# Four of down's low weight parts formed on GpSimd, and four reorderings ahead of them, in a decoder layer

## The chip, the cores and the metric

The kernel runs on one core of a Trainium2 chip. The metric is the device time of one execution in microseconds (us); the kernel before took 369.11 us in the median of three runs (368.17 to 369.8). A core has a matrix engine (TensorE, in the rows PE, its weight loads PEld), a vector engine (VectorE, DVE), a scalar engine (ScalarE, ACT), GpSimd (POOL) and a queue engine (SyncE, SP) that issues most DMAs. Each engine executes its own instructions in program order and waits on semaphores for the others.

## The reference

One layer over x (256 tokens x 1024), in float32:

```
z = x @ w_in;  u = z[:, :512];  q, k, v = thirds of z[:, 512:]     # 8 heads of 64
pool = causal window means of u (2, 4, 8, 16) - u, times w_pool, times pool_scale
attn = causal softmax(q k^T / 8) v
h1 = layer_norm(a*x + concat(pool, attn) @ w_out)                  # a = 2^(1/4)
cross = softmax((h1 @ w_xq) (mem @ w_xk)^T / 16) (mem @ w_xv)      # 4 heads of 256, 256 memory tokens
h2 = layer_norm(a*h1 + cross @ w_xo)
out = layer_norm(a*h2 + (silu(h2 @ w_gate) * (h2 @ w_up)) @ w_down)  # inner width 2816
```

## The kernel before

**Three products for one.** TensorE multiplies in a float32 form of fewer bits (F32R). So each operand is kept as two parts: a high part, which ScalarE casts, and a low part, which VectorE forms as the operand minus its high part. A product is three matmuls: high by high, high by low, low by high (`three`, L353 to L358). A matmul of 128x512 or 128x256 outputs adds into one of eight PSUM banks: a ring of four for long accumulations (`accbank`) and a ring of four for the rest (`bank`). A bank comes free when the engine that reads its former content has done so.

**The weight stream.** All weights pass through one `Stream`, as numbered items (w0 to w138) in the order of use. For an item SyncE's queue loads a raw tile (7 buffers), ScalarE casts the high part (L146, L160) and VectorE subtracts the low part (L148, L161); high and low tiles have 9 buffers. The program order on ScalarE, VectorE and SyncE is fixed when the kernel is built: every call of `ws.get` in the generator of a projection first makes sure that its own item is prepared, and, unless `ws.held` is set, prepares one item more, up to 9 ahead of what is used. With `ws.pace` at n only every n-th call does so. A raw buffer is loaded anew only after its low part has been formed, and the load stands in SyncE's order right behind the preparation that frees it.

**The stages, in order.** q and k (w0 to w10), v, u, the keys of the memory (`do_xk`, w19 to w26), the output projection `mix` (w27 to w34) with the first layer norm, the values of the memory (`do_xv`, w35 to w42), the four heads of cross-attention (`do_xq`, `xscores`, `xattend`), their output projection with the second layer norm, eleven chunks of gate and up (`proj_n`, c = 0 to 10), and down. The generators yield after each step of k, and `run(gen, n)` takes n steps, so that the softmax, pooling and splits of other parts are put between them by hand.

**Keys of the memory.** `do_xk` makes four chunks in 64 steps, and after each chunk splits the accumulator into xkT (ScalarE, then VectorE, through `split`, L418 to L420). The bank of its last chunk is the one in which the fourth accumulator of `mix` begins. The last steps stand so:

```
run(xk, 6)        # L688
mix_pool(2)
mix_pool(3)
run(xk, 6)
run(xk)
```

**Scores of a head.** `xscores` (L847) makes for two token halves and two slices of the head the three products each, in the order high by high, high by low, low by high; the low part of the query is written by VectorE (`split_scaled`, L424).

**First gate/up chunk.** Before chunk 0 the tokens of h2 are turned on TensorE and split into h2T; `proj_n` (L380) for the first token half begins as soon as that is there.

**Down.** For the first 9 of 11 chunks (SEVEN = 9) down is done on two-by-two blocks with seven products instead of eight: weight sums (`sums`) and token sums (GpSimd, L968 to L973) are formed, four products are shared over the chunks (`shared_products`) and three are added on (`four`, `fourth`). After the last gate/up chunk `down` runs: the single-row weights w121 to w134 (`c_t4`, `c_low`), then the last two chunks, w135 to w138, for each of the four output pieces in turn (L1154 to L1156). The pieces 1 and 2 get the shared sums added by VectorE before they begin (L1144). In between `events` puts the splits of the last tokens and the merging of the shared sums (L1116 to L1125). The third layer norm and the stores follow.

Of the kernel before, what the change touches and what calls it, by code (L numbers as in the profile page):

```python
# [14 lines left out]
P = 128  # L15
D = 1024
S = 256
T = S // P
KD = D // P
# [16 lines left out]
SEVEN, LAG, LATE = 9, 2, 4  # L36


def r32(t):
    return t.bitcast(F32)  # L40


class Stream:


    def __init__(self, nc, pool):
        self.nc, self.pool = nc, pool
        self.src, self.raws, self.tiles, self.homes = [], [], [], []
        self.loads, self.splits = {}, {}
        self.used, self.held = 0, True  # L50
        self.pace, self.asked = 1, 0
        self.cuts, self.steps = {}, {}
        self.items, self.freed, self.rest = [], 0, {}
        self.kept = set()

    def add(self, src, parts=2):

# [71 lines left out]
    def prepare(self, upto, now=False):  # L129
        nc = self.nc  # L130
        while len(self.tiles) < min(upto, len(self.items)):
            i = len(self.tiles)
            kind, r = self.items[i]
            if kind == "sums" and upto < i + 2 and not now:
                break
            for split in self.splits.pop(i, []):
                split()
            if kind == "whole":
                self.fetch(r + 1, nc.sync)
                raw = self.raws[r]  # L140
                hi = self.pool.tile(list(raw.shape), F32R, tag="hi", name=f"w{i}h")
                lo = self.pool.tile(list(raw.shape), F32R, tag="lo", name=f"w{i}l")
                whole = [slice(0, raw.shape[2])]
                casts, subs = self.steps.get(r, (whole, whole))
                for s in casts:
                    nc.scalar.copy(hi[:, :, s], raw[:, :, s])  # L146
                for s in subs:
                    nc.vector.tensor_sub(lo[:, :, s], raw[:, :, s], r32(hi[:, :, s]))  # L148
                self.tiles.append((hi, lo))
                self.freed = r + 1  # L150
            elif kind == "sums":
                self.fetch(r + 2, nc.sync)
                self.tiles += self.sums(i, r)
                self.freed = r + (1 if r in self.kept else 2)
            else:
                raw, (hi, lo) = r(), self.part(i)
                self.freed += len(self.kept)
                self.kept.clear()
                s = slice(0, raw.shape[2])
                nc.scalar.copy(hi[:, :, s], raw)  # L160
                nc.vector.tensor_sub(lo[:, :, s], raw, r32(hi[:, :, s]))  # L161
                self.tiles.append((hi, lo))
            self.fetch(max(self.freed, len(self.homes)) + RAW_BUFS, nc.sync)

    def next(self):

        i = len(self.tiles)
        return i + (2 if i < len(self.items) and self.items[i][0] == "sums" else 1)
# [28 lines left out]
def decoder_layer(  # L197
# [3 lines left out]
    nc = tc.nc  # L201
# [11 lines left out]
    def a8(name, dt=F32):  # L213
        return ap.tile([P, KD, S], dt, tag="a8", name=name)

    def bank(name):
        return pb.tile([P, 512], F32, tag="b", name=name)

    def accbank(name):
        return pa.tile([P, 512], F32, tag="acc", name=name)  # L220


    ws = Stream(nc, wp)
# [8 lines left out]
    def block(w, at, shape):  # L232

        j, n = shape
        return w[at:at + P * j * n].rearrange("(p j n) -> p j n", p=P, j=j)

    c_qk = []
    for k in range(KD):
        if k < 3:
            first = [ws.add(block(w_qkv, (2 * k + j) * P * 512, (1, 512)), 1)[0] for j in range(2)]  # L240
# [13 lines left out]
    def row(k):  # L254

        return w_down[k * P:(k + 1) * P].rearrange("(k p) n -> p k n", p=P)
# [10 lines left out]
    c_gu, c_sums = [], []  # L267
    for c in range(NFC):
        c_gu.append(ws.add(w_gu[c], 4))
        n = c - LAG  # L270
        if 0 <= n < SEVEN:
            c_sums.append(ws.add_sums([row(2 * n), row(2 * n + 1)], (lambda n=n: t4_home(n)) if n < SEVEN - 1 else None))
    c_t4, c_low = {}, {}
    c_t4[SEVEN - 1] = ws.add_home(lambda: ws.rest[ws.items[c_sums[-1][0][0]][1]]())
    c_low[SEVEN - 1] = ws.add(row(2 * SEVEN - 1), 1)
    for n in range(0, SEVEN - 1, 2):
        home = lambda n=n: t4[n // 2]
        if n < LATE:
            c_t4[n] = ws.add_home(home)
        for c in (n, n + 1):  # L280
            c_low[c] = ws.add(row(2 * c + 1), 1)
        if n >= LATE:
            c_t4[n] = ws.add_home(home)
    c_dn = {c: [ws.add(row(2 * c + f), 1) for f in range(2)] for c in range(SEVEN, NFC)}


# [66 lines left out]
    def three(ps, w, y, start, stop, part=False):  # L353

        (wa, wb), (ya, yb) = w, y
        nc.tensor.matmul(ps, wa, ya, start=start, stop=False, skip_group_check=part)  # L356
        nc.tensor.matmul(ps, wa, yb, start=False, stop=False, skip_group_check=part)  # L357
        nc.tensor.matmul(ps, wb, ya, start=False, stop=stop, skip_group_check=part)  # L358

    def pair(hl, *ix):  # L360
        return hl[0][ix], hl[1][ix]

    ALL = slice(None)
# [13 lines left out]
                    ws.done(numbers, k)  # L377
                yield

    def proj_n(pss, numbers, yT, last=True):  # L380

        for k in range(KD):
            for t, ps in pss.items():
                three(ps, pair(yT, ALL, k, slice(t * P, (t + 1) * P)), ws.get(numbers, k), k == 0, k == KD - 1)
            if last:
                ws.done(numbers, k)
            yield
# [22 lines left out]
    def run(gen, n=None):  # L410

        while n is None or n > 0:
            if next(gen, gen) is gen:
                return False
            n = None if n is None else n - 1
        return True
# [201 lines left out]
    def mix_pool(g):  # L618
        pm = bank("pm")
        nc.tensor.matmul(pm[:, :S], wpl[:, g, :], upad[:, g, PADW:], start=True, stop=True)  # L620
        nc.scalar.activation(cT[0][:, g, :], pm[:, :S], AF.Copy, bias=0.0, scale=psc[:, g:g + 1])
        nc.vector.scalar_tensor_tensor(cT[1][:, g, :], pm[:, :S], psc[:, g:g + 1],
                                       r32(cT[0][:, g, :]), op0=OP.mult, op1=OP.subtract)


    def do_v():
        pieces = [(t, 0, 512) for t in range(T)]
        acc = {piece: accbank("pv") for piece in pieces}
        yield from proj_rows(acc, c_v, lambda k: (xT[0][:, k], xT[1][:, k]), pieces, True, True, True)
        for piece in pieces:  # L630
            nc.scalar.copy(vt[:, piece[0], :], acc[piece])

    def do_u():
        for c in range(2):
            ps = accbank("pu").rearrange("p (f t) -> p f t", f=2)
            yield from proj_t([ps[:, f, :] for f in range(2)], c_u[c], xT)
            nc.scalar.copy(upad[:, 2 * c:2 * c + 2, PADW:], ps)
            for f in range(2):
                windows(2 * c + f)

    xkT = (a8("xkTh", F32R), a8("xkTl", F32R))

    def do_xk():
        for c in range(4):
            ps = accbank("pxk").rearrange("p (f t) -> p f t", f=2)
            yield from proj_t([ps[:, f, :] for f in range(2)], c_xk[c], mT)
            split(xkT[0][:, 2 * c:2 * c + 2, :], xkT[1][:, 2 * c:2 * c + 2, :], ps)

    v, u, xk = do_v(), do_u(), do_xk()
# [38 lines left out]
    run(xk, 6)  # L688
    mix_pool(2)
    mix_pool(3)  # L690
    run(xk, 6)
    run(xk)
    ws.pace = 1


# [56 lines left out]
    PIECES = tuple((t, *half) for t in range(T) for half in HALVES)  # L752
# [62 lines left out]
    xv = [ap.tile([P, T, D], F32R, tag="a8", name=f"xv{i}") for i in range(2)]  # L815

    def do_xv():
        acc = {piece: (bank if piece == PIECES[3] else accbank)("xv") for piece in PIECES}
        yield from proj_rows(acc, c_xv, lambda k: (mT[0][:, k], mT[1][:, k]),
                             PIECES, True, True, True)  # L820
        xvs.update(acc)
# [17 lines left out]
    xqT, xpr, xpt, turnsx = {}, {}, {}, {}  # L839
# [6 lines left out]

    def xscores(h):  # L847
        ps = bank("xs").rearrange("p (t s) -> p t s", t=2)
        for t in range(T):
            for kk in range(2):  # L850
                three(ps[:, t, :], pair(xqT[h], ALL, kk, slice(t * P, (t + 1) * P)), pair(xkT, ALL, 2 * h + kk),
                      kk == 0, kk == 1)
        pr = sp.tile([P, 2, T, P], F32, name="xpr", tag="pr", bufs=PR_BUFS)
        by_t = pr.rearrange("p s t b -> p t s b")
        scaled(by_t, exps(by_t, ps.rearrange("p t (s b) -> p t s b", s=2), negmax(ps)))
        xpr[h] = pr
# [68 lines left out]
    h2T = (a8("h2Th", F32R), a8("h2Tl", F32R))  # L925
# [94 lines left out]
    first = [accbank("pg") for t in range(T)]  # L1020
    second = [accbank("pg") for t in range(T)]
    gu1 = [proj_n({t: second[t]}, c_gu[1], h2T, t == 1) for t in range(T)]
    run(proj_n({0: first[0]}, c_gu[0], h2T, False))
    transpose_tok(h2T, h2[:, 1, :], 1, 0)
    run(gu1[0], 2)
    gated(0, 0, first[0])
# [11 lines left out]
    acc = {}  # L1038
# [8 lines left out]
    for c in range(1, NFC):  # L1047
        sgs.append(sp.tile([P, 2, T, P], F32, name="sg", tag="pr", bufs=PR_BUFS))
        pss = {t: second[t] if c == 1 else accbank("pg") for t in range(T)}
# [236 lines left out]
```

## Time and profile before

| | |
|---|---|
| median of three runs | 369.11 us (368.17 to 369.8) |
| the profiled execution | 369.07 us, span of its instructions 367.1 us |
| TensorE busy | 361.8 us, 99% of the span |
| VectorE busy | 309.8 us, 84% |
| ScalarE busy | 198.4 us, 54% |
| GpSimd busy | 68.1 us, 19% |
| granted TensorE clock | full (1.0, the level of 2.4 GHz) over the span |

The span is the time from the first to the last instruction of the program; the execution's own time has 1.9 us more around it. A timeline row gives start and duration of an instruction in us, the engine, the line of the kernel, the operation, output<-inputs, shapes, and in brackets the idle time of the engine just before it and what ended that. Matmuls are pipelined: durations overlap, and the step from one start to the next is what a matmul costs, 0.23 us for 128x512 and 0.12 us for 128x256. Vector instructions overlap a little too: a low part of 128x1024 lasts 1.22 us, and the next starts 1.13 us after it.

### The profile page before, as it was taken

To read this page: it belongs to the slowest core of one execution; us is meant where nothing else is said; L and a number is where in the kernel's file an instruction comes from. 1 tells how busy PE (TensorE), PEld (TensorE's weight loads), DVE (VectorE), ACT (ScalarE), POOL (GpSimd) and SP (SyncE) were. 2 spreads that over 40 slices of the span, in tenths; PEclk is the share of its full clock that TensorE was granted. 3 is DMA by queue.
4 is the path that set the end of the run, shared out by engine and by line. 5 is a ranking of instruction groups with operands and counts; after the bars stand their busy time and mean duration, and the time that the engine had idled before them with its cause. 6 is when DMAs were issued, how large, how long until landed. Compare 5 with 4: busy or idle time off the path is not lost.

```text
span 367.1 us, 5725 instructions
## 1 busy us (share of the span) xinstructions
PE 361.8 (99%) x1999; PEld 312.9 (85%) x1999; DVE 309.8 (84%) x461; ACT 198.4 (54%) x303; POOL 68.1 (19%) x102
## 2 busy tenths in 40 slices
PE   9999999999999999999999999999999999999995
PEld 9997999996888899988888888888888888888884
DVE  5868897995599796775788989999998999879974
ACT  5656863952253465554328438546565664679301
POOL 1000039240010003320010024044314404400000
PEclk9999999999999999999999999999999999999999
DMA  7997599689815996854104896797879778657311
GB/s 251 417 422 296 203 312 316 220 247 363 302 65 173 337 393 225 298 175 178 57 0 148 312 369 229 237 341 259 311 259 339 242 233 319 228 187 239 107 47 67
DMA packets 33980, 89.24 MB, mean 243 GB/s; under 512 B 4256, under 2 KB 12576, under 8 KB 33824
## 3 DMA queue, kind: packets, MB, share of 16 engines
q1 hardware_dynamic: 31664, 83.77, 64.7%
q0 software_dynamic: 1712, 4.72, 4.0%
q10 hardware_dynamic: 576, 0.39, 0.3%
q8 instruction: 15, 0.25, 0.3%
q14 instruction: 13, 0.11, 0.1%
HBM read 81.53 MB, written 7.34 MB: 242 GB/s over the span
## 4 chain that ended last, share of the span: by engine, by line
PE 82%; issue 12%; DVE 3%; DMA 1%; POOL 1%; ACT 0%; POOLq 0%; ACTq 0%; DVEq 0%
PE pg L358 11%; PE pg L356 11%; PE pg L357 11%; PE pqk L493 6%; PE pxk L374 6%; PE acc L356 5%; PE acc L357 5%; PE acc L358 5%; PE pu L374 3%; PE x L358 2%; PE x L356 2%; PE x L357 2%; DMA xd<-xs 1%; PE pv L356 1%; PE acc L1155 1%
## 5 line engine op out<-in xcount | busy, mean ns | idle before, releaser
L968 POOL TENSOR_TENSOR sraw<-gr 128x128 f32<-128x128 f32 x9 | 9.0, 1003 | 94.6 <-DMA gr<-gd 69.5
L730 POOL TENSOR_TENSOR rs<-mv,mhalf 128x1 f32<-128x1 f32 x6 | 3.8, 640 | 97.5 <-DVE mv L728 97.5
L530 ACT ACTIVATE pr<-pr,mx 128x128 f32<-128x128 f32 (+1 forms) x16 | 7.1, 445 | 10.0 <-DVE mx L561 10.0
L443 POOL DMA_DIRECT2D pd<-ps x4 | 2.4, 612 | 48.2 <-DVE ps L440 47.9
L451 POOL DMA_DIRECT2D pt<-pd x16 | 8.8, 554 | 8.7 <-ACT w23h L146 3.8
L419 ACT CAST h2Th<-tp 128x512 fp32r<-128x512 f32 x4 | 2.3, 586 | 14.6 <-PE tp L430 14.6
L969 POOL TENSOR_TENSOR sraw<-sraw,gr 128x128 f32<-128x128 f32 x9 | 9.6, 1072 | 0.7
L948 ACT ACTIVATE sg<-pg 128x256 f32<-128x256 f32 x22 | 7.9, 381 | 3.0 <-PE pg L358 3.0
L970 POOL TENSOR_TENSOR sraw<-gr 128x128 f32<-128x128 f32 x9 | 9.0, 1005 | 0.0
L419 ACT CAST gTh<-gr 128x512 fp32r<-128x512 f32 x11 | 6.8, 615 | 3.6 <-DMA gr<-gd 3.6
L949 DVE TENSOR_TENSOR sg<-sg,pg 128x256 f32<-128x256 f32 x22 | 8.4, 414 | 0.1
L420 DVE TENSOR_TENSOR gTl<-gr,gTh 128x512 fp32r<-128x512 f32 x11 | 8.3, 754 | 0.0
L451 POOL DMA_DIRECT2D xr<-xd x12 | 6.5, 551 | 8.5 <-PE xs L357 2.9
L443 POOL DMA_DIRECT2D xd<-xs x3 | 1.7, 576 | 34.2 <-DVE xs L440 34.2
L440 DVE STREAM_TRANSPOSE gs<-sg 128x512 f32<-128x512 f32 x11 | 7.7, 701 | 0.1
L530 ACT ACTIVATE xpr<-xs,mx 128x256 f32<-128x256 f32 x8 | 3.7, 470 | 7.0 <-DVE mx L541 7.0
L419 ACT CAST S<-sraw 128x384 fp32r<-128x384 f32 (+1 forms) x9 | 4.7, 522 | 4.6 <-POOL sraw L970 4.6
L735 DVE SCALAR_TENSOR_TENSOR r<-r,mv,g 128x512 f32<-128x512 f32 (+1 forms) x10 | 7.0, 730 | 0.2
L1206 ACT ACTIVATE minus<-ident 128x128 f32<-128x128 f32 x1 | 0.3, 311 | 12.1 <-DVE r L741 12.1
L721 DVE BATCH_NORM_STATS2 st<-r 128x6 f32<-128x512 f32 (+1 forms) x10 | 6.4, 641 | 0.3
L535 DVE RECIPROCAL sm<-sm 128x2 f32<-128x2 f32 x12 | 2.0, 164 | 5.6 <-ACT xpr L530 4.3
L973 POOL TENSOR_TENSOR S<-gr,sraw 128x128 f32<-128x128 f32 x8 | 6.6, 829 | 0.0
(1396 smaller groups left out, 1507.6 us busy)
## 6 DMA issues: line engine op xcount, KB each, us to landing
gd<-gs SPq DMA_DIRECT2D x11, 256.0 KB, 5.5
gr<-gd SPq DMA_DIRECT2D x44, 64.0 KB, 2.0
pd<-ps POOLq DMA_DIRECT2D x4, 384.0 KB, 4.3
pt<-pd POOLq DMA_DIRECT2D x16, 96.0 KB, 7.2
g<-in_ln_g SPq DMA_DIRECT2D x3, 512.0 KB, 4.9
b<-in_ln_b SPq DMA_DIRECT2D x3, 512.0 KB, 6.0
wr<-in_w_qkv SPq DMA_DIRECT2D x5, 256.0 KB, 4.3
mr<-in_mem_t SPq DMA_DIRECT2D x1, 1024.0 KB, 11.9
```

The costliest lines, as they stand in the source:

```text
L356: nc.tensor.matmul(ps, wa, ya, start=start, stop=False, skip_group_check=part)
L357: nc.tensor.matmul(ps, wa, yb, start=False, stop=False, skip_group_check=part)
L358: nc.tensor.matmul(ps, wb, ya, start=False, stop=stop, skip_group_check=part)
L374: nc.tensor.matmul(pss[f], w[:, s], y, start=k == 0 and f == 0 and n == 0, stop=k == KD - 1 and n == 2, skip_group_check=True)
L419: nc.scalar.copy(h, ps)
L451: queue.dma_start(raw[32 * j:32 * (j + 1)].rearrange("p i m b -> p i (m b)"), via[:, j, :].rearrange("(i a) r -> a i r", i=4))
L493: nc.tensor.matmul(qk[i][:, f, :], w[:, c * P:(c + 1) * P], y, start=k == 0 and f == 0 and w is hi and y is x_hi, stop=k == KD - 1 and w i ...
L530: nc.scalar.activation(dst[:, j, :], src[:, j, :], AF.Exp, bias=mx[:, j:j + 1], scale=sign, accum_out=sm[:, j:j + 1])
L949: nc.vector.tensor_mul(sg, sg, ps[:, CW:].rearrange("p (f b) -> p f b", f=2))
L968: nc.gpsimd.tensor_add(s1, a21, a22)
L969: nc.gpsimd.tensor_sub(s2, s1, a11)
L970: nc.gpsimd.tensor_sub(s3, a11, a21)
```

## The change

Five edits. (1) `ws.third` holds four items, the low weight rows of chunks 1, 3, 5 and 7 of down; by the order of the items these are w125, w128, w130 and w133. Their low parts are formed by GpSimd instead of VectorE, with the same instruction at the same place of the program. (2) In the last 18 steps of `do_xk` preparation ahead is held for the last 9. (3) In `do_xv` the third of four accumulators, not the fourth, gets its bank from the ring of the rest. (4) `xscores` makes all eight products with the high part of the query first and the four with its low part last. (5) The first `proj_n` puts the low products of its first two steps behind the high ones.

```diff
@@ Stream
-        self.kept = set()
+        self.kept, self.third = set(), set()
...
+                engine = nc.gpsimd if i in self.third else nc.vector
                 for s in subs:
-                    nc.vector.tensor_sub(lo[:, :, s], raw[:, :, s], r32(hi[:, :, s]))
+                    engine.tensor_sub(lo[:, :, s], raw[:, :, s], r32(hi[:, :, s]))
...
+    ws.third = {c_low[c][0] for c in range(1, SEVEN - 1, 2)}
@@ proj_n
-    def proj_n(pss, numbers, yT, last=True):
-
+    def proj_n(pss, numbers, yT, last=True, late=0):
+
+        behind = []
         for k in range(KD):
             for t, ps in pss.items():
-                three(ps, pair(yT, ALL, k, slice(t * P, (t + 1) * P)), ws.get(numbers, k), k == 0, k == KD - 1)
+                y, w = pair(yT, ALL, k, slice(t * P, (t + 1) * P)), ws.get(numbers, k)
+                if k >= late:
+                    three(ps, y, w, k == 0, k == KD - 1)
+                    continue
+                for n in range(2):
+                    nc.tensor.matmul(ps, y[0], w[n], start=k == n == 0, stop=False)
+                behind.append((ps, y[1], w[0]))
+            if k == late - 1:
+                for ps, y, w in behind:
+                    nc.tensor.matmul(ps, y, w, start=False, stop=False)
@@ the last steps of do_xk
-    run(xk, 6)
+    run(xk, 9)
+    ws.held = True
     run(xk)
+    ws.held = False
     ws.pace = 1
@@ do_xv
-        acc = {piece: (bank if piece == PIECES[3] else accbank)("xv") for piece in PIECES}
+        acc = {piece: (bank if piece == PIECES[2] else accbank)("xv") for piece in PIECES}
@@ xscores
-        for t in range(T):
-            for kk in range(2):
-                three(ps[:, t, :], pair(xqT[h], ALL, kk, slice(t * P, (t + 1) * P)), pair(xkT, ALL, 2 * h + kk),
-                      kk == 0, kk == 1)
+        for low in range(2):
+            for t in range(T):
+                for kk in range(2):
+                    w = xqT[h][low][:, kk, t * P:(t + 1) * P]
+                    for n in range(2 - low):
+                        nc.tensor.matmul(ps[:, t, :], w, xkT[n][:, 2 * h + kk], start=not (low or t or kk or n),
+                                         stop=bool(low and kk), skip_group_check=True)
@@ gate and up, chunk 0
-    run(proj_n({0: first[0]}, c_gu[0], h2T, False))
+    run(proj_n({0: first[0]}, c_gu[0], h2T, False, 2))
```

## Rows read from the trace of the kernel before

**Rows 1.** The page: busy time of each engine.

```profile
PE 361.8 (99%) x1999; PEld 312.9 (85%) x1999; DVE 309.8 (84%) x461; ACT 198.4 (54%) x303; POOL 68.1 (19%) x102
```

**Rows 2.** All waits of PE: total us, times, longest us.

```profile
PE busy L463 <- PEq L1250: 0.8, 1, 0.8
PE acc L356 <- DVE xkTl L420: 0.6, 1, 0.6
PE xs L358 <- DVE xq L424: 0.3, 1, 0.3
```

**Rows 3.** Timeline of PE, beginning of `mix`: start, duration.

```profile
82.71 0.39 PE L358 MATMUL acc<-w27h,cTl 128*128 128x512 f32 x1
83.65 0.50 PE L356 MATMUL acc<-w27h,cTh 128*128 128x512 f32 x1 [0.55 <-DVE xkTl L420]
```

**Rows 4.** Timeline of DVE, the same place.

```profile
80.66 1.21 DVE L148 TENSOR_TENSOR w33l<-w33r,w33h 128x1024 fp32r<-128x1024 f32 x1
81.79 1.21 DVE L148 TENSOR_TENSOR w34l<-w34r,w34h 128x1024 fp32r<-128x1024 f32 x1
82.92 0.68 DVE L420 TENSOR_TENSOR xkTl<-pxk,xkTh 128x512 fp32r<-128x512 f32 x1
```

**Rows 5.** Timeline of ACT, the same place.

```profile
81.07 0.59 ACT L419 CAST xkTh<-pxk 128x512 fp32r<-128x512 f32 x1 [1.90 <-PE pxk L374]
```

**Rows 6.** Timeline of PE, scores of the last head.

```profile
156.33 0.28 PE L357 MATMUL xs<-xkTl,xq 128*128 128x256 f32 x1
156.92 0.39 PE L358 MATMUL xs<-xkTh,xq 128*128 128x256 f32 x1 [0.31 <-DVE xq L424]
```

**Rows 7.** Timeline of DVE, the same place.

```profile
155.08 1.18 DVE L148 TENSOR_TENSOR w58l<-w58r,w58h 128x1024 fp32r<-128x1024 f32 x1
156.19 0.68 DVE L424 SCALAR_TENSOR_TENSOR xq<-pxq,xq 128x512 fp32r<-128x512 f32 x1
```

**Rows 8.** Timeline of PE, third product of gate/up chunk 0.

```profile
186.24 0.50 PE L358 MATMUL pg<-w59h,h2Tl 128*128 128x512 f32 x1
```

**Rows 9.** Timeline of POOL, window sums of the pooling.

```profile
57.60 0.22 POOL L611 TENSOR_TENSOR win<-win,fac 128x16 f32<-128x16 f32 x1
59.45 0.64 POOL L609 TENSOR_TENSOR win<-upad 128x271 f32<-128x271 f32 x1
```

**Rows 10.** Timeline of POOL, token sums beside VectorE's low parts.

```profile
305.57 1.45 POOL L970 TENSOR_TENSOR sraw<-gr 128x128 f32<-128x128 f32 x1
306.98 0.46 POOL L973 TENSOR_TENSOR S<-gr,sraw 128x128 f32<-128x128 f32 x1
```

**Rows 11.** Timeline of DVE, the same place.

```profile
303.81 1.48 DVE L148 TENSOR_TENSOR w116l<-w116r,w116h 128x1024 fp32r<-128x1024 f32 x1
305.21 1.48 DVE L148 TENSOR_TENSOR w117l<-w117r,w117h 128x1024 fp32r<-128x1024 f32 x1
307.88 1.23 DVE L148 TENSOR_TENSOR w118l<-w118r,w118h 128x1024 fp32r<-128x1024 f32 x1 [0.57 <-ACT w118h L146]
```

**Rows 12.** A stretch: length; busy (count) PE, PEld, DVE, ACT, POOL; clock; DMA.

```profile
330.00:349.00 19.00, 19.00 (x86) 15.73 (x85) 18.62 (x21) 13.20 (x16) 0.00 (x0) 1.00 0.54 167
```

**Rows 13.** Timeline of DVE in that stretch: two low parts, the adds into acc.

```profile
331.57 1.22 DVE L148 TENSOR_TENSOR w128l<-w125r,w128h 128x1024 fp32r<-128x1024 f32 x1
...
346.52 1.22 DVE L148 TENSOR_TENSOR w138l<-w133r,w138h 128x1024 fp32r<-128x1024 f32 x1
347.66 1.29 DVE L1144 TENSOR_TENSOR acc<-u,acc 128x512 f32<-128x512 f32 x2
```

**Rows 14.** Timeline of PE: first use of w128l, of w138l, of piece 1.

```profile
340.10 0.39 PE L357 MATMUL acc<-w128l,gTh 128*128 128x512 f32 x1
...
348.94 0.39 PE L1155 MATMUL acc<-w138l,gTh 128*128 128x512 f32 x1
...
349.39 0.39 PE L1154 MATMUL acc<-w135h,gTh 128*128 128x512 f32 x1
```

**Rows 15.** Timeline of SP's queue: the last gated tokens are fetched.

```profile
334.38 2.81 SPq L451 DMA_DIRECT2D gr<-gd  x4
```

## The prediction

> **What bounds the kernel now.** The page's busy times come first [rows 1]: TensorE is busy for 361.8 of 367.1 us, VectorE for 309.8. So nothing is gained off TensorE unless TensorE waits for it, and the second view is the list of TensorE's own waits [rows 2]. Beside the start-up it has two entries: one on VectorE's xkTl where `mix` begins, one on VectorE's xq in the scores of a head. Third come the timelines of both places, where the reader sees what stands ahead of the late instruction on VectorE [rows 3 to 7]. Fourth is the stretch in which edit 1 works, 330 to 349 us [rows 12]: TensorE runs through it without a gap, VectorE is busy for 18.62 of 19 us, GpSimd not at all. There TensorE waits for nobody, but VectorE has almost no room left.
>
> The sum is made against the profiled execution, 369.07 us, 0.04 under the median of 369.11. What lies outside the span (1.97 us) the change does not touch.
>
> **Edit 2 (held preparation).** By the rule of the stream the only item whose preparation falls in the nine held steps is w34; it moves behind the split of the last chunk. Before, w34l at 81.79 stands ahead of xkTl, which starts at 82.92 [rows 4], although its high part was there at 81.07 + 0.59 = 81.66 [rows 5]. After, xkTl takes w34l's place, starts 1.13 earlier and ends at about 82.47. TensorE's fourth accumulator, due at 82.71 + 0.23 = 82.94, began at 83.65, and that matmul lasted 0.50 instead of 0.39 [rows 3]: 0.71 + 0.11 = 0.82 us go, with 0.47 to spare. What is late next is nothing nearby: w34 is first used 57 products of 0.23 us, 13 us, after `mix` begins, and the load that waits for its raw buffer moves by the same 1.1 us. Without that cover the cost would be one low part, 1.13 us.
>
> **Edit 4 (scores).** The third product came at 156.92 instead of 156.33 + 0.12 and lasted 0.39 instead of 0.28 [rows 6]: 0.47 + 0.11 = 0.58 us. It needs the low part of the query, ready at 156.19 + 0.68 = 156.87 [rows 7]. After, the first product with it is the ninth, six products of 0.12 us later, at 157.17, so 0.3 us to spare: all 0.58 goes. The number of matmuls stays. The open point is whether the low part comes earlier when TensorE does: it stands behind w58l and a chain that began in the scores of the head before, so I take it that it moves along; if it did not move at all, edit 2's 0.82 would eat the 0.3 and 0.52 of the gain. Bounds 0.06 and 0.58, taken 0.58.
>
> **Edit 5.** One product waited for the low part of h2T: 0.50 instead of 0.39 [rows 8], 0.11 us. Two low products move behind four high ones; bounds 0 and 0.11, taken 0.11.
>
> **Edit 3.** TensorE's list has no wait at the values [rows 2], so nothing can be gained there; what it could cost is bounded by the three products of 0.23 us (0.68 us) that change places with respect to the release of a bank. VectorE reads both accumulators one after the other as before. Taken 0.
>
> In front: 0.82 + 0.58 + 0.11 = 1.51 us less. Behind these places the work of the other engines starts from TensorE's results (norms, gated tokens, splits), so the whole rest moves along.
>
> **Edit 1 (four low parts on GpSimd).** It takes four subtractions of 1.13 us each (from start to start [rows 4]) out of VectorE's order. As TensorE waits for none of them, taking them out is worth nothing by itself. What they do on GpSimd decides. Where GpSimd adds 128 elements beside VectorE's low parts, those last 1.48 instead of 1.23 us [rows 11], 0.25 us each, and GpSimd's addition lasts 1.45 instead of 0.46 [rows 10] and ends at 307.02, 0.33 after w117l's end at 306.69. So the two take turns: GpSimd reads only between two such VectorE instructions, and the next one waits until GpSimd has read. I call that a hold; it is the duration alone less 0.21 (0.46 - 0.25).
>
> The Trainium skill has the same as a rule (SBUF — State Buffer, section "Who interferes with whom"): a VectorE instruction with two inputs in SBUF and a GpSimd instruction that reads SBUF shut each other out for the whole of the one that came first. By that rule moving a subtraction from the one to the other relieves VectorE of nothing, and the trace agrees with the 0.25 us above.
>
> No row shows GpSimd at 1024 elements. From contiguous rows: 0.22 us at 16 elements and 0.64 at 271 [rows 9] make 1.65 ns an element, so 1.88 us, a hold of 1.67. From the strided token sums: 0.46 at 128 [rows 10] against 0.22 at 16 make 2.14 ns an element, so 2.38 us, a hold of 2.17. Below, a hold that costs VectorE nothing is not excluded by a row of this size. A weight row is contiguous, so I stay near the first and take 1.8.
>
> Place by place. w125l comes before the dense stretch and is used some 11 us later; I count 0, and 0.67 if VectorE is tight there. w128l, w130l and w133l lie in the stretch: each swaps 1.13 us of VectorE's own time for a hold of 1.8, +0.67, in all +2.01 us on w138l and on the additions into the accumulators, which end the full order [rows 13]. w138l ends at 347.74 and is needed at 348.94 [rows 14], 1.20 to spare; the first addition (half of the 1.29) ends at about 348.31 and piece 1 begins at 349.39, 1.08 to spare. So TensorE stands 2.01 - 1.08 = 0.93 us before piece 1. At the ends: 3 x (1.67 - 1.13) - 1.08 = 0.54 and 3 x (2.17 - 1.13) - 1.08 = 2.04; with no hold 0.
>
> The moved parts themselves are in time: w128l starts where w127l ends (331.57), is done at about 333.6 and needed at 340.10 [rows 14]; w130 and w133 are used 12 and 24 products (2.7 and 5.4 us) after it and follow on GpSimd two holds and low parts later, at about 336.5 and 339.6. Behind them on GpSimd only the power of the last norms waits. On SyncE's queue the load into w128's raw buffer and what stands behind it wait up to 1 us longer, the fetch of the last gated tokens (334.38 [rows 15]) among them; those are used at 348, so nothing follows.
>
> Sum: 369.07 - 1.51 + 0.93 = 368.5 us.
>
> The Trainium skill gives 4497 ns for such an addition of 2048 elements (GPSIMD Engine Reference, section "3.1 Elementwise — side-by-side cycle accounting"); half of it, an estimate, is 2.25 us, a hold of 2.04, and the sum by it would be 369.07 - 1.51 + 1.65 = 369.2. No run here shows it yet.
>
> **The rivals.** (A) VectorE is truly relieved: GpSimd's reads fall into gaps or hold VectorE no longer than the subtraction did, and only the front counts: 369.07 - 1.51 = 367.6. For it: GpSimd is idle in the stretch [rows 12], and 1.08 us of spare absorb holds up to 1.49. Against it: the 1.48 us rows.
>
> (B) The other side: the hold is long, and TensorE stands before w138l and piece 1 for more than the front gave. It decides from 3 x (H - 1.13) - 1.08 = 1.51, H = 1.99 us; below that the kernel is not slower. At the strided end, 2.17, the time is 369.07 - 1.51 + 2.04 = 369.6; at 2.8, should the rounded output cost a half more than the contiguous rows let expect, 369.07 - 1.51 + 3.93 = 371.5. For it: the token sums' price per element. Against it: the contiguous rows.
>
> (C) The edits in front do not do what they say: the query's low part does not come earlier with TensorE, 0.52 of the gain is lost, and with the 0.93 of edit 1 the time is 369.0. For it: VectorE's order ahead of it is full [rows 7]. Against it: that order starts from TensorE's own results.
>
> **How the numbers follow.** Forecast 0.43 (its own range 367.9 to 369.1), A 0.27, B 0.20, C 0.10. The prediction is the forecast's 368.5. The range takes in A's time with the spread of the runs shown (about 0.6 below it) and B up to a hold of about 2.5: 367.0 to 370.6. A difference of 0.5% (1.85 us) is about what a measurement can tell from no change: faster needs less than 367.26, which only A's lower edge reaches, 0.16; slower needs more than 370.96, the upper part of B, 0.14; the rest is 0.70.
>
> **What would show it.** In TensorE's waits the entries on xkTl and xq are gone, and xkTl stands directly behind w33l. GpSimd has four rows of 128x1024, alone about 2.0 us long. VectorE's low parts beside them (w129l, w131l, and S or w132l) last about 2.9 us instead of 1.22. w138l ends later against TensorE's first product of w135 than before, and TensorE has a new wait of about 0.9 us before w138l's product or piece 1. If those low parts keep 1.22 us, A is right; if the wait is over 1.5 us, B is. I am wrong in the front if a new wait of 0.3 us or more stands between 84 and 330 us.

## The result, and the profile after

The changed kernel takes 371.68 us (median of 6 runs, 370.25 to 372.74) against 368.92 us before (6 runs): 1.007 times as long, with a 95% interval of 1.0049 to 1.0091. It became slower, 2.8 us by the medians, where 368.5 us was forecast. Its profiled span is 369.0 us, 1.9 more than before.

The page's busy times of the changed kernel, which answer to [rows 1]: GpSimd has 13.6 us more, but VectorE, with four instructions fewer, has 2.4 us more too.

```profile
PE 362.7 (98%) x1999; PEld 313.0 (85%) x1999; DVE 312.2 (85%) x457; ACT 197.7 (54%) x303; POOL 81.7 (22%) x106
```

All of TensorE's waits in the changed kernel (total us, times, longest us; for [rows 2]). The two entries on xkTl and xq are gone; three on VectorE's low parts of the last weights are new.

```profile
PE acc L1172 <- DVE w138l L149: 1.4, 1, 1.4
PE busy L475 <- PEq L1267: 0.8, 1, 0.8
PE acc L1172 <- DVE w136l L149: 0.3, 1, 0.3
PE acc L1172 <- DVE w137l L149: 0.2, 1, 0.2
```

The timeline of TensorE at that place, before (one row) and after (start, duration; for [rows 14]). Between the starts of w136h and w136l lie 0.69 us instead of 0.23, before w137l 0.57, before w138l 1.77: 0.46 + 0.34 + 1.54 us. After each wait, and at the first product of piece 1, a matmul lasts 0.50 instead of 0.39 us, four times 0.11. Together 2.8 us.

```profile
346.67 0.39 PE L1154 MATMUL acc<-w135h,gTh 128*128 128x512 f32 x1
```

```profile
345.70 0.39 PE L1171 MATMUL acc<-w135h,gTh 128*128 128x512 f32 x1
...
346.38 0.39 PE L1171 MATMUL acc<-w136h,gTh 128*128 128x512 f32 x1
347.07 0.50 PE L1172 MATMUL acc<-w136l,gTh 128*128 128x512 f32 x1 [0.30 <-DVE w136l L149]
...
347.64 0.40 PE L1171 MATMUL acc<-w137h,gTh 128*128 128x512 f32 x1
348.21 0.50 PE L1172 MATMUL acc<-w137l,gTh 128*128 128x512 f32 x1 [0.17 <-DVE w137l L149]
...
348.77 0.40 PE L1171 MATMUL acc<-w138h,gTh 128*128 128x512 f32 x1
350.54 0.51 PE L1172 MATMUL acc<-w138l,gTh 128*128 128x512 f32 x1 [1.37 <-DVE w138l L149]
...
351.14 0.50 PE L1171 MATMUL acc<-w135h,gTh 128*128 128x512 f32 x1
```

Where VectorE lost this is seen in two timelines. GpSimd's four rows (start, duration): the first begins while VectorE is idle and takes 2.40 us; the third and fourth last 1 us longer, as they begin beside a low part of VectorE that has yet to end.

```profile
323.27 2.40 POOL L149 TENSOR_TENSOR w125l<-w123r,w125h 128x1024 fp32r<-128x1024 f32 x1 [3.81 <-DMA gd<-gs]
330.94 2.50 POOL L149 TENSOR_TENSOR w128l<-w125r,w128h 128x1024 fp32r<-128x1024 f32 x1 [5.26 <-ACT w128h L146]
333.39 3.39 POOL L149 TENSOR_TENSOR w130l<-w127r,w130h 128x1024 fp32r<-128x1024 f32 x1
336.74 3.39 POOL L149 TENSOR_TENSOR w133l<-w129r,w133h 128x1024 fp32r<-128x1024 f32 x1
```

VectorE beside them, before and after (for [rows 11 and 13]). The first S lasts 2.48 us instead of 0.69, w129l 2.68 instead of 1.22, w131l 3.42 instead of 1.22, the later S 2.89 instead of 0.69. The last two stood for 2.20 us each. w129l stood for 1.46 us, after 0.67 us of idle time in which ScalarE's high part of w129 was not there yet; GpSimd was reading in that time too. From the start of w127l to the end of w138l it is 20.54 us; before, w127l began at 330.43 and w138l ended at 347.74 [rows 13], 17.31 us.

```profile
325.34 0.69 DVE L420 TENSOR_TENSOR S<-sraw,S 128x512 fp32r<-128x512 f32 x1
...
330.43 1.23 DVE L148 TENSOR_TENSOR w127l<-w124r,w127h 128x1024 fp32r<-128x1024 f32 x1 [0.33 <-ACT w127h L146]
...
332.70 1.22 DVE L148 TENSOR_TENSOR w129l<-w126r,w129h 128x1024 fp32r<-128x1024 f32 x1
...
334.97 1.22 DVE L161 TENSOR_TENSOR w131l<-t,w131h 128x1024 fp32r<-128x1024 f32 x1
336.11 0.69 DVE L420 TENSOR_TENSOR S<-S,S 128x512 fp32r<-128x512 f32 x1
```

```profile
323.75 2.48 DVE L432 TENSOR_TENSOR S<-sraw,S 128x512 fp32r<-128x512 f32 x1 [1.41 <-ACT S L431]
...
327.89 0.74 DVE L966 TENSOR_TENSOR sg<-sg,pg 128x256 f32<-128x256 f32 x2
...
329.94 1.23 DVE L149 TENSOR_TENSOR w127l<-w124r,w127h 128x1024 fp32r<-128x1024 f32 x1 [0.57 <-DMA gr<-gd]
331.84 2.68 DVE L149 TENSOR_TENSOR w129l<-w126r,w129h 128x1024 fp32r<-128x1024 f32 x1 [0.67 <-ACT w129h L146]
334.44 3.42 DVE L162 TENSOR_TENSOR w131l<-t,w131h 128x1024 fp32r<-128x1024 f32 x1
337.78 2.89 DVE L432 TENSOR_TENSOR S<-S,S 128x512 fp32r<-128x512 f32 x1
...
349.27 1.21 DVE L149 TENSOR_TENSOR w138l<-w133r,w138h 128x1024 fp32r<-128x1024 f32 x1
```

The balance of the two profiled executions: TensorE reaches the first product of w135 at 345.70 instead of 346.67, 0.97 us earlier, and the identity products after the last piece at 362.31 instead of 360.43, 1.88 us later. Between them lie the 2.8 us of new waits.

### The profile page after: what moved, and what is told of

Same layout as the page of the kernel before. It is cut to its first block, busy times and chain, and to the rows that moved or that the text cites. A ratio compares the mean times of both kernels' runs of the same rounds, so it can differ in the third digit from the quotient of the medians.

```text
span 369.0 us, 5726 instructions
## 1 busy us (share of the span) xinstructions
PE 362.7 (98%) x1999; PEld 313.0 (85%) x1999; DVE 312.2 (85%) x457; ACT 197.7 (54%) x303; POOL 81.7 (22%) x106
## 4 chain that ended last, share of the span: by engine, by line
PE 89%; DMA 3%; DVE 3%; issue 1%; ACT 1%; SPq 1%; POOL 1%; DVEq 0%; POOLq 0%
PE pg L360 10%; PE pg L359 10%; PE pg L358 10%; PE pqk L505 6%; PE pxk L376 6%; PE pxq L376 6%; PE acc L358 4%; PE acc L359 4%; PE acc L360 4%; PE pu L376 3%; DMA gr<-gd 2%; PE xv L360 2%; PE xv L358 2%; PE xv L359 2%; PE x L358 2%; PE x L359 2%
## 5 line engine op out<-in xcount | busy, mean ns | idle before, releaser
L985 POOL TENSOR_TENSOR sraw<-gr 128x128 f32<-128x128 f32 x9 | 9.3, 1031 | 93.2 <-DMA gr<-gd 57.3
L987 POOL TENSOR_TENSOR sraw<-gr 128x128 f32<-128x128 f32 x9 | 9.5, 1055 | 0.0
L432 DVE TENSOR_TENSOR S<-sraw,S 128x384 fp32r<-128x384 f32 (+1 forms) x9 | 6.9, 764 | 2.3 <-ACT S L431 2.3
L990 POOL TENSOR_TENSOR S<-gr,sraw 128x128 f32<-128x128 f32 x8 | 7.6, 949 | 0.0
```

Of the source, the lines that this page charges most:

```text
L432: nc.vector.tensor_sub(l, ps, r32(h))
L985: nc.gpsimd.tensor_add(s1, a21, a22)
L987: nc.gpsimd.tensor_sub(s3, a11, a21)
```

## The experiments

The theory T: a GpSimd subtraction holds VectorE for 2.2 us where VectorE's own took 1.13; the stretch has about 1.1 us of spare; the rest goes to TensorE. The rivals: F, a reordering costs; R, GpSimd's results or the loads behind them come late; W, any GpSimd work on the memory holds VectorE, not its reading alone. Ratios are to the kernel before on the same chip.

**The reorderings alone.** `ws.third` is left empty.

```diff
-    ws.third = {c_low[c][0] for c in range(1, SEVEN - 1, 2)}
```

> The four reorderings without the GpSimd rows. Theory T (GpSimd's subtractions hold VectorE 2.2 us each in a stretch where VectorE is full, and everything else is gain): 1.3 us under the kernel before (0.82 + 0.38 + 0.11), about 367.6 us, and TensorE's waits on xkTl and on w136l, w137l, w138l gone. Rival F (a reordering itself costs, at the banks or in the scores): 369.5 us or more, with a new wait between 84 and 205 us.

Measured: 367.8 us against 368.2 (11 and 25 runs), 0.9992 (0.9983 to 1.0001). F falls: there is no loss in front, and TensorE waits for nobody after the start-up, which is the whole list here:

```profile
PE busy L474 <- PEq L1266: 0.8, 1, 0.8
```

But 0.3 us (0 to 0.6) is a quarter of the 1.3 us that T expected. The profiled span, 365.9, is 1.2 us under that of the kernel before; the timed runs don't show it. The experiments on the hop below show one reason: the trace of the kernel before has a wait that not every execution has.

**The GpSimd rows alone**, on the kernel before.

```diff
+        self.kept, self.third = set(), set()
...
+                engine = nc.gpsimd if i in self.third else nc.vector
-                    nc.vector.tensor_sub(lo[:, :, s], raw[:, :, s], r32(hi[:, :, s]))
+                    engine.tensor_sub(lo[:, :, s], raw[:, :, s], r32(hi[:, :, s]))
...
+    ws.third = {c_low[c][0] for c in range(1, SEVEN - 1, 2)}
```

> The kernel before with the four GpSimd rows alone. T: VectorE falls back by 0.5 us at w125 and by 3 x (2.2 - 1.13) = 3.2 us in the dense stretch, less 1.2 us of spare, and three restarts of 0.1: TensorE stands some 2.8 us, about 371.7 us. F: 369 us or less, since the loss would come from the reorderings.

Measured: 371.8 us against 368.2, 1.0098 (1.0084 to 1.0112), 3.6 us (3.1 to 4.1). The whole loss belongs to edit 1. It is 0.8 us more than T's 2.8, from four runs, and no row accounts for the difference. TensorE's waits on w136l, w137l and w138l are the same three; beside them this trace has a wait of 0.6 us in the start-up, on ScalarE's high part of w2:

```profile
PE acc L1157 <- DVE w138l L149: 1.4, 1, 1.4
PE busy L465 <- PEq L1252: 0.8, 1, 0.8
PE pqk L495 <- ACT w2h L146: 0.6, 1, 0.6
PE acc L1157 <- DVE w136l L149: 0.3, 1, 0.3
PE acc L1157 <- DVE w137l L149: 0.2, 1, 0.2
```

**One row, two rows, the first row**, each with the reorderings.

```diff
-    ws.third = {c_low[c][0] for c in range(1, SEVEN - 1, 2)}
+    ws.third = {c_low[5][0]}                  # one row: w130
+    ws.third = {c_low[3][0], c_low[5][0]}     # two rows: w128, w130
+    ws.third = {c_low[1][0]}                  # the first row: w125
```

> The four reorderings and one GpSimd row, w130, in the dense stretch. T: one hold in place of one subtraction, 1.07 us, which the spare of 1.1 to 1.2 us just covers: 0 to 0.3 us over the reorderings alone, about 367.7 us. Rival R (a GpSimd part is late for TensorE or for the loads behind it): every row costs alike, about a quarter of the loss of all four, 0.7 us or more over the reorderings alone.

> The four reorderings and two GpSimd rows, w128 and w130. T: 2.14 us of delay on VectorE less 1.2 of spare, with restarts 1.0 to 1.2 us over the reorderings alone, about 368.7 us, and TensorE waits for VectorE's w138l, not for GpSimd. R: half of the loss of all four, 1.5 to 2 us, and TensorE's wait stands on GpSimd or a load.

> The four reorderings and one GpSimd row, w125, ahead of the dense stretch. T: VectorE falls back by some 0.5 us there, inside the spare of 1.1 us at the end of the stretch: no cost, 367.8 us, no new wait of TensorE. R: a quarter of the loss of all four, 0.7 us or more over the reorderings alone.

Measured: one row 368.25 us, 1.0001 (0.9992 to 1.001); two rows 369.15, 1.0026 (1.0016 to 1.0035), both against 368.2; the first row 0.9992 (0.997 to 1.0015). Over the reorderings alone in the same session, one row costs 0.45 us and two cost 1.35, where T said 0 to 0.3 and 1.0 to 1.2. The first row costs nothing that shows. The times alone do not part T from R: R's 0.7 us a row is not clear of the intervals of the one row and the first row. The traces part them. VectorE's stretch from the start of w127l to the end of w138l grows by T's 1.07 us, within 0.01, for every row in it, and by nothing for w125, whose row stands ahead of it:

| GpSimd rows | w127l's start to w138l's end | what TensorE shows |
|---|---|---|
| none | 17.32 us | w138l is there 1.19 us ahead of its first product |
| w125 | 17.32 us | 0.71 us ahead |
| w130 | 18.40 us | 0.11 us ahead |
| w128, w130 | 19.48 us | a wait of 0.9 us |
| all four | 20.54 us | waits of 1.4, 0.3 and 0.2 us |

So the delay goes by the row, and TensorE's loss begins when the delay exceeds the spare. VectorE's rows with one row, then with two:

```profile
329.68 1.23 DVE L149 TENSOR_TENSOR w127l<-w124r,w127h 128x1024 fp32r<-128x1024 f32 x1 [0.33 <-ACT w127h L146]
...
346.87 1.21 DVE L149 TENSOR_TENSOR w138l<-w133r,w138h 128x1024 fp32r<-128x1024 f32 x1
```

```profile
328.97 1.23 DVE L149 TENSOR_TENSOR w127l<-w124r,w127h 128x1024 fp32r<-128x1024 f32 x1 [0.33 <-ACT w127h L146]
...
347.24 1.21 DVE L149 TENSOR_TENSOR w138l<-w133r,w138h 128x1024 fp32r<-128x1024 f32 x1
```

With one row the list of TensorE's waits has nothing beyond the start-up, but the first product with w138l lasts 0.44 instead of 0.39 us, and this and the steps behind it lose 0.2 of the 0.45 us; the rest is not tied to a row of the trace. With two rows TensorE's only wait past the start-up stands on VectorE, not on GpSimd or a load:

```profile
PE acc L1172 <- DVE w138l L149: 0.9, 1, 0.9
```

**GpSimd writing, and GpSimd reading, beside VectorE.** VectorE keeps all low parts; at the four places GpSimd does extra work that nobody needs.

```diff
+                if i in self.third:
+                    # the writing kernel
+                    nc.gpsimd.tensor_sub(self.scratch[:, :, :1], raw[:, :, :1], r32(hi[:, :, :1]))
+                    for _ in range(4):
+                        nc.gpsimd.memset(self.scratch, 0.0)      # 480 elements
+                    # the reading kernel, in its place
+                    for c in (0, 480):
+                        s = slice(c, c + 480)
+                        nc.gpsimd.tensor_sub(self.scratch, raw[:, :, s], r32(hi[:, :, s]))
...
-                    engine.tensor_sub(lo[:, :, s], raw[:, :, s], r32(hi[:, :, s]))
+                    nc.vector.tensor_sub(lo[:, :, s], raw[:, :, s], r32(hi[:, :, s]))
```

> The four reorderings; VectorE forms all low parts itself, and beside each of the same four GpSimd reads one element and then fills a scratch tile of 480 elements four times with zeros (about 2 us of writing), which nobody reads. T (the hold is GpSimd's reading of two inputs against VectorE's two): no cost, 367.8 us as with the reorderings alone, and the low parts beside it stay at 1.22 us. Rival W (any GpSimd work on that memory holds VectorE, as long as it lasts): 3 x 2 - 1.1, about 5 us over, 372.5 us or more.

> As the kernel with the writes, but beside each of the four low parts GpSimd subtracts twice 480 elements of the same two inputs into the scratch tile. Nobody waits for these results. T: each holds VectorE for about 1.0 us without taking anything off it: three places in the dense stretch, 6.0 us less 1.1 of spare and with restarts some 5 us over the reorderings alone, about 373 us; the low parts beside it last over 2 us. Rival R (the loss came from GpSimd's results or loads being late, not from VectorE standing): 0 to 0.5 us over.

Measured: writing 0.9994 (0.9976 to 1.0011), as the reorderings alone; reading 376.7 us against 369.19, 1.0195 (1.0159 to 1.023). W falls. So does R as the cause of the loss: nobody waits for GpSimd's results here, and the time goes up all the same. VectorE's rows in the writing kernel, and GpSimd's beside them: 2.17 us of filling, and the low part keeps its 1.22 us.

```profile
331.56 1.22 DVE L152 TENSOR_TENSOR w128l<-w125r,w128h 128x1024 fp32r<-128x1024 f32 x1
332.69 1.22 DVE L152 TENSOR_TENSOR w129l<-w126r,w129h 128x1024 fp32r<-128x1024 f32 x1
```

```profile
331.75 2.17 POOL L150 MEMSET scratch<- 128x480 f32 x4
```

The same in the reading kernel: each low part stands 1.02 us for a subtraction of 480 elements, and the two engines go by turns.

```profile
333.57 2.25 DVE L152 TENSOR_TENSOR w128l<-w125r,w128h 128x1024 fp32r<-128x1024 f32 x1
335.75 2.24 DVE L152 TENSOR_TENSOR w129l<-w126r,w129h 128x1024 fp32r<-128x1024 f32 x1
```

```profile
333.47 3.44 POOL L150 TENSOR_TENSOR scratch<-w125r,w128h 128x480 f32<-128x480 f32 x2 [4.70 <-issue]
```

The Trainium skill says the same (SBUF — State Buffer, section "Who interferes with whom"): a VectorE instruction with two inputs in SBUF collides with a GpSimd instruction that reads SBUF, not with one that only writes it. The two kernels agree, with 2.24 against 1.22 us. The loss, 7.9 us over the writing kernel, was larger than the 5 us that T gave, since the first place counts as well: its two holds moved w127l from 330.42 in the writing kernel to 332.43, and the six in the stretch add 6.1 us.

**Where the gain in front went.** The kernel before once more, for a second trace; and two kernels in which the fetches of the first probabilities no longer stand ahead of the first window sums on GpSimd's queue, on the kernel before and on the reorderings alone.

```diff
-    run(u, 4)
+    run(u, 10)
     probs_in(0)
     probs_in(1)
-    run(u, 6)
     split_mem(4)
```

> The kernel before once more, for its trace. Theory V (the wait on xkTl is no fixed part of an execution: VectorE stood 1.5 us before the pooling's difference, because GpSimd's window sums stood behind fetches that waited for the landing of a hop through DRAM): VectorE's idle time before that difference is another one than 1.49 us, and TensorE's wait on xkTl moves with it, down to none. Rival: 1.4 to 1.6 us again and a wait of 0.7 to 0.9 us.

> The kernel before, with the fetches of the first two heads' probabilities put on GpSimd's queue behind the window sums of the first pooling chunk instead of ahead of them. Theory V (the wait on xkTl hangs on the landing of that hop): VectorE's idle time before the pooling's difference is 0.3 us or less, TensorE has no wait on xkTl, and the time is 0 to 0.5 us under the kernel before. Rival (the wait belongs to w34l's place alone): xkTl's wait stays in the trace.

> The same move on top of the four reorderings without GpSimd rows. V: nothing more is to be had at xkTl, so the time is that of the reorderings alone, 0.3 to 0.6 us under the kernel before. Rival: if both waits were independent, another 0.8 us less.

The second trace of the kernel before (span 366.6) has no wait on xkTl:

```profile
PE busy L463 <- PEq L1250: 0.8, 1, 0.8
PE xs L358 <- DVE xq L424: 0.4, 1, 0.4
```

What differs is a landing. GpSimd's fetches of the second head stand behind a write of the probabilities to DRAM; in the first trace of the kernel before GpSimd was idle for 2.13 us until it had landed, and VectorE then 1.49 us until the window sums were there (GpSimd's row, then VectorE's):

```profile
54.68 2.17 POOL L451 DMA_DIRECT2D pt<-pd  x4 [2.13 <-DMA pd<-ps]
```

```profile
57.86 0.84 DVE L616 SCALAR_TENSOR_TENSOR upad<-win,upad 128x256 f32<-128x256 f32 x1 [1.49 <-POOL win L611]
```

In the second trace GpSimd's idle time is 0.44 us, and VectorE's is too short for its row to print:

```profile
53.83 2.17 POOL L451 DMA_DIRECT2D pt<-pd  x4 [0.44 <-DMA pd<-ps]
```

```profile
57.08 0.84 DVE L616 SCALAR_TENSOR_TENSOR upad<-win,upad 128x256 f32<-128x256 f32 x1
```

From there VectorE's order is full up to xkTl, which comes at 82.13 instead of 82.92 although TensorE is 0.2 us later in that trace. In the ten other traces with this order of GpSimd's queue its idle time there is 0 to 1.33 us, so the 2.13 us of the first trace is the longest. The kernel with the GpSimd rows alone, which keeps w34l ahead of xkTl, has no wait there either, but in its trace TensorE is also 1.0 us later from the start-up on, so it does not single out the landing. With the window sums first, neither wait is listed (on the kernel before, the third score product still comes 0.29 us late), and the time is 1.0011 (0.999 to 1.0031) on the kernel before and 0.9993 (0.9981 to 1.0004) on the reorderings, where TensorE gets a new wait of 0.4 us on the fetch that now comes later. So the landing explains the two traces; that the move by itself makes the kernel faster is not shown. The move has a price, by T: the window sums now run beside VectorE's low parts, which last 1.67 instead of 1.23 us (VectorE's row, then GpSimd's):

```profile
48.34 1.67 DVE L148 TENSOR_TENSOR w21l<-w21r,w21h 128x1024 fp32r<-128x1024 f32 x1
```

```profile
47.78 1.14 POOL L609 TENSOR_TENSOR win<-upad 128x271 f32<-128x271 f32 x1 [0.73 <-ACT upad L637]
```

Such a sum lasts 0.64 us in [rows 9], and 0.64 - 0.21 is 0.43: the prediction's rule for a hold again, at 271 elements.

**The changed kernel once more.**

> The changed kernel once more, timed with the others. T: the loss of the GpSimd rows alone (3.6 us) less what the reorderings gave (0.3 us in the timed runs): 3.3 us, about 0.9%, over the kernel before, with VectorE's low parts beside GpSimd again 2.7 to 3.4 us long.

Measured: 371.2 us against 368.82, 1.008 (1.0058 to 1.0103), 2.4 us by the medians. VectorE's rows beside GpSimd last 2.69, 3.43 and 2.89 us. The interval holds the expected 0.9%.

No kernel beat the one before clearly. The four with the reorderings and without GpSimd rows in the dense stretch or extra reading came to 0.9992 to 0.9994, each with an interval that holds 1.

## Why the prediction was wrong

The mechanism was the predicted one; the step that failed is the sum 369.07 - 1.51 + 0.93, in both its terms. The 0.93 us that TensorE was to stand for edit 1 measured 2.8 us: the hold was larger than taken, w125l was put at nothing, and the longer matmuls behind the new waits were left out. The 1.51 us that the front was to give were 1.31 in the profiled execution, 0.97 with a longer start-up, and 0.3 in the timed runs.

**The hold, "so I stay near the first and take 1.8".** It was 2.20 us, and outside both ends that rows gave (1.67 and 2.17). The rule for it held: the duration alone less 0.21 is 2.40 - 0.21 = 2.19. What failed was the length at 1024 elements: the contiguous rows made 1.88 us, the strided ones 2.38, and 2.40 was measured. The end that was nearer in layout was the wrong one. Rows at 16 and 271 elements do not fix a slope for 1024. Three holds make 3 x (2.20 - 1.13) = 3.21 us, and the delay of w138l behind w127l was 20.54 - 17.31 = 3.23. The estimate of 2.25 us, half of what the Trainium skill gives for 2048 elements (GPSIMD Engine Reference, section "3.1 Elementwise — side-by-side cycle accounting"), lay nearer than the value taken; the trace shows 2.40 us.

**w125l, "I count 0".** It held the first S for 1.8 us. VectorE's gated product and ScalarE's casts follow that, so w127l began 0.49 us earlier than before while TensorE was 0.97 us earlier: 0.48 us lost, where 0.67 was named as the price without cover. In the kernel with that row alone the spare takes it.

**The spare of 1.20 and 1.08 us** was right as a size: 3.23 + 0.48 - 1.20 is 2.5 us. The trace has w138l's first product 2.57 us later against the first of w135 than before. Two of the four longer matmuls come behind that, 0.2 us; they were counted at the waits that go but not at the ones that come. That is the 2.8 us of TensorE, where 0.93 was forecast.

**The front, 1.51 us.** In the profiled execution edit 2 gave its 0.82 and edit 5 its 0.11. Edit 4 gave 0.38 of 0.58. VectorE's xq came 0.17 us earlier while TensorE came 0.50 earlier, and the first product with the low part still waited (0.22 instead of 0.12 us to the next, and another 0.1 after it):

```profile
156.54 0.28 PE L868 MATMUL xs<-xkTl,xq 128*128 128x256 f32 x1
156.76 0.51 PE L868 MATMUL xs<-xkTh,xq 128*128 128x256 f32 x2
```

That is rival C in part, and it too goes by the execution: from the first score product to the product behind the scores it is 1.63 us here, but 1.44, the full gain, in five of the nine traces with edit 4, and 1.63 to 2.10 in the four without (2.01 in the one that was forecast from). A start-up 0.33 us longer took some back (v began at 27.80 instead of 27.47; over all traces it began at 27.28 to 28.46); 0.82 + 0.38 + 0.11 - 0.33 is the 0.97, within rounding. In the timed runs the front is worth 0.3 us. One reason is that the wait that edit 2 removes, more than half of the sum, is in the trace forecast from and in none of the three others without edit 2; how often it comes in timed runs is not shown. Edit 3 moved nothing that a trace shows.

**The rivals.** B was right in mechanism and side: it decides at a hold of 1.99 us, and the hold was over that. By its formula 2.20 us gives 369.07 - 1.51 + 2.13 = 369.7; the other 2 us are the front's 1.2, w125's 0.5 and the longer matmuls. (B's 2.8 us for a rounded output, a half more than the contiguous rows' 1.88 us, is a duration; by the prediction's own rule the hold would be 2.6.) With all of that known, 368.92 - 0.3 + 2.8 is 371.4, against 371.68. A is refuted by the 1.02 us of each reading, and by w129l and w131l.

## What to carry to other kernels

Moving a two-input subtraction from a full VectorE to an idle GpSimd relieves VectorE of nothing here: it swaps 1.13 us of its own work for a hold of 2.20 us. Where a price is bounded by two slopes from small sizes, keep both until the size is measured, and count the moved work at each place by what stands behind it there. A wait in one profiled execution may be an event of that execution: follow it back to what released it, and where that is a landing in DRAM, count it in part until a second trace shows it.

## What was not expected of the hardware

GpSimd's subtraction of 1024 elements took 2.40 us alone, 0.64 us at 271: 2.34 ns an element between them, against 1.65 between 16 and 271. A fill of 480 elements took 0.54 us, and the low part beside it kept its 1.22 us. After each wait, TensorE's next matmul of 128x512 lasted 0.50 instead of 0.39 us, whether the wait was 1.37 or 0.17 us, and the one behind it began 0.34 instead of 0.23 us later. GpSimd stood 2.13 and 0.44 us for the landing of the same write to DRAM in two executions of the same kernel; from the end of the write's issue to the fetch behind it were 8.2 and 7.1 us. The start-up, up to the first product of v, took 27.28 to 28.46 us in the thirteen traces.
